# Moving chunk 0's choice of experts from the scatter stage into the dense stage of a hybrid block with product-key experts

## Chip, cores and metric

One NeuronCore of a Trainium2 chip. The metric is the device time of one execution in microseconds; three executions of the kernel before took 1862.81 to 1864.69 us, median 1863.86.

## The reference

One block on 512 tokens of width 1024, in float32: a recurrent branch and an attention branch, mixed and added, and then a layer of 16384 experts addressed by product keys (PEER). The last is what matters here:

```python
def one_chunk(xt):                                  # 128 tokens
    q = (xt @ w_q).reshape(BLOCK, PEER_HEADS, PEER_QDIM)
    s1 = jnp.einsum('chd,nd->chn', q[..., :half], keys1)
    s2 = jnp.einsum('chd,nd->chn', q[..., half:], keys2)
    t1, i1 = lax.top_k(s1, PEER_TOPK)               # 16 of 128
    t2, i2 = lax.top_k(s2, PEER_TOPK)
    cand = t1[..., :, None] + t2[..., None, :]      # 256 candidates
    cidx = i1[..., :, None] * PEER_NKEYS + i2[..., None, :]
    ts, sel = lax.top_k(cand, PEER_TOPK)            # 16 of them
    idx = jnp.take_along_axis(cidx, sel, axis=-1)
    g = jax.nn.softmax(ts, axis=-1)
    act = jax.nn.gelu(jnp.einsum('chkd,cd->chk', u[idx], xt))
    return jnp.einsum('chk,chkd->cd', g * act, v[idx])
```

Each token takes 8 heads x 16 = 128 experts. There are four chunks of 128 tokens. A final norm follows.

## The kernel before

The chunks are handled in the order 1, 2, 3, 0 (`ORDER`). Three of them (1, 2, 3; `NDC = 3`) go through all experts densely: for each of 128 blocks of 128 experts (`NJ`), a u block (24 matmuls of 384 columns, float32 split into a high and a low part) gives activations for 384 tokens, these are multiplied by a matrix of gates, and 18 matmuls with the v block add to six banks `y`. Chunk 0 goes by index: for each of its 128 experts a token the rows of u and then of v are fetched by an indirect DMA on the POOL queue (`fetch`, L913), 128 rows of 4 KB at a time, and VectorE multiplies each with the normed tokens (`first_by_index`, L926) or adds it to `acc` (`second_by_index`, L935). A "row" below is one such fetch and its VectorE operation.

Before the dense stage stand:

- `key_scores` (L724), 16 query products, the top 16 of 128 keys for all four chunks, into `tv` and `ti`;
- `choose` (L757), once per chunk: candidates (a fixed set of 50 pairs of ranks), their top 16 for each of 8 heads (L787 to L791, five operations with a load of match values ahead of three of them), the indices of these by masks (L803 comparison, L805 product, L806 sum), and the gates (L809 difference, L810 Exp on ScalarE, L812 to L814). It is a generator with twelve pieces;
- `scatter` (L843), once per dense chunk: it turns indices and gates into the matrix of gates in DRAM, `gd`, with comparisons on VectorE (L879, L884), scaling on ScalarE (L888), and 128x128 products on TensorE (L869).

`interleave` (L107) runs generators side by side by their weights: each in turn goes on that has used the smallest share of its number of pieces. Scatter of chunk i runs beside the choice of chunk i + 1 and beside u blocks done ahead (`first_ahead`, 41 blocks, `LAG`). Here a scheduler may still move instructions; in the dense stage the context `in_order` keeps VectorE's instructions in the order in which they are written.

In the dense stage `dense` (L971) runs beside the chain of `first_by_index` and `second_by_index`. In step j it first calls `stage(j + 1)` (L952): the u block j + 1 + 41 (two halves, cast on ScalarE L155, difference on VectorE L156; three buffers for what arrives and four for the parts), the v tile (L155, L156; two buffers), and the coefficients `gt`, `ch`, `cl` (L965, L155, L156). Then come the u block's matmuls and the 18 of step j. It yields 4 for a step with a u block (87 of them) and 1 for one without (41); the index chain yields 1 a row, 264 in all. Row buffers: four of 128 x 1024 (`GB = 4`).

```python
yield 1 if w is None else 4
interleave((dense(), 4 * NJ - 3 * LAG), (chain(first_by_index(0), second_by_index(0, acc)), 2 * NS + 2 + GE))
```

Of the kernel before, what the change touches and what calls it, by code (L numbers as in the profile page):

```python
# [19 lines left out]
P = 128  # L20
D = 1024
# [22 lines left out]
NJ = 128  # L44
LAG = 41
# [4 lines left out]
NDC = 3  # L50
# [51 lines left out]
def chain(*gens):  # L102
    for g in gens:
        yield from g


def interleave(*gens):  # L107

    items = [[g, n, 0] for g, n in gens if n]
    while items:  # L110
        it = min(items, key=lambda i: i[2] / i[1])
        try:
            it[2] += next(it[0]) or 1
        except StopIteration:
            items.remove(it)
# [3 lines left out]
def hybrid_block_kernel(ctx: ExitStack, tc, hT, x, win, wkr, vecs, wgate, wrnn, watt, wuq, wukv, wout,  # L119
                        wq, keysT, g2, gf, peer_u, peer_uT, peer_v, cst, out):  # L120
    nc = tc.nc
    V, A, G, TE = nc.vector, nc.scalar, nc.gpsimd, nc.tensor

    def pool(stack, name, side="left", **kw):
        return stack.enter_context(tc.tile_pool(name=name, bufs=1, side=side, reuse_waits="tile", **kw))
# [11 lines left out]
    right = ExitStack()  # L137
# [12 lines left out]
    efx = [cp.tile([P, NS], F32, name=f"efx{c}") for c in range(4)]  # L150
    gate = [cp.tile([P, NS], F32, name=f"gate{c}") for c in range(4)]
# [215 lines left out]
    for hb in range(NK // HB):  # L367
# [47 lines left out]
        ks = [slice(k, k + 1) for k in range(hb * HB, hb * HB + HB)]  # L415
# [297 lines left out]

    dx = ExitStack()
    ctx.enter_context(dx)
    actp = pool(dx, "act", "right")
    vp = pool(dx, "vstream", "right")
    po_ = pool(postx, "choice")
    scx = ExitStack()
    sp_ = pool(scx, "scat", "right")  # L720
    tv = [po_.tile([P, PH, 2, TOPK], F32, name=f"tv{i}") for i in range(4)]
    ti = [po_.tile([P, PH, 2, TOPK], U32, name=f"ti{i}") for i in range(4)]

    def key_scores():  # L724

# [28 lines left out]
            V.max(t[:, 8:16], sv)  # L754
            V.max_index(u[:, 8:16], t[:, 8:16], sv)

    def choose(i, c):  # L757

        work = po_.tile([P, 2 * PH * NCAND], F32, tag="work", bufs=1, name=f"work{c}")
        tf = work[:, PH * NCAND:PH * NCAND + 2 * P].rearrange("p (h a k) -> p h a k", h=PH, a=2)  # L760
        V.tensor_copy(tf, ti[i])
        V.tensor_scalar(tf[:, :, 0, :], tf[:, :, 0, :], float(P), None, op0=OP.mult)
        cd = work[:, :PH * NCAND].rearrange("p (h n) -> p h n", h=PH)
        cx = po_.tile([P, PH, NCAND], F32, tag="cx", bufs=1, name=f"cx{c}")

        def outer(dst, src, a0, na, b0, nb):
            V.tensor_add(dst.rearrange("p h (a b) -> p h a b", b=nb),
                         src[:, :, 0, a0:a0 + na].unsqueeze(3).to_broadcast([P, PH, na, nb]),
                         src[:, :, 1, b0:b0 + nb].unsqueeze(2).to_broadcast([P, PH, na, nb]))

        p0 = 0
        for a0, na, nb in ((0, 1, 16), (1, 1, 8), (2, 1, 5), (3, 1, 4), (4, 1, 3), (5, 3, 2), (8, 8, 1)):
            outer(cd[:, :, p0:p0 + na * nb], tv[i], a0, na, 0, nb)
            p0 += na * nb
            if a0 == 2:
                yield
        yield
        p0 = 0
        for grp in PAIRS:
            for a0, na, b0, nb in grp:  # L780
                outer(cx[:, :, p0:p0 + na * nb], tf, a0, na, b0, nb)
                p0 += na * nb
        yield
        ts = po_.tile([P, PH, TOPK], F32, tag="ts", bufs=1, name=f"ts{c}")
        sel = po_.tile([P, PH, TOPK], U32, tag="sel", bufs=1, name=f"sel{c}")
        for h in range(PH):
            V.max(ts[:, h, 0:8], cd[:, h, :])  # L787
            V.max_index(sel[:, h, 0:8], ts[:, h, 0:8], cd[:, h, :])
            V.match_replace(out=cd[:, h, :], in_to_replace=ts[:, h, 0:8], in_values=cd[:, h, :], imm_value=NEG)
            V.max(ts[:, h, 8:16], cd[:, h, :])  # L790
            V.max_index(sel[:, h, 8:16], ts[:, h, 8:16], cd[:, h, :])  # L791
            if h % 2:
                yield
        sf = po_.tile([P, PH, TOPK], BF16, tag="sf", bufs=1, name=f"sf{c}")
        V.tensor_copy(sf, sel)
        ef = efx[c].rearrange("p (h k) -> p h k", h=PH)
        n = 0
        for g, grp in enumerate(PAIRS):
            n += sum(na * nb for a0, na, b0, nb in grp)
            ks = slice(4 * g, 4 * g + 4)  # L800
            oh = po_.tile([P, PH, 4, NCAND], F32, tag="oh", bufs=1, name=f"oh{c}_{g}")[:, :, :, :n]
            ob = work.bitcast(BF16)[:, :PH * n * 4].rearrange("p (h n k) -> p h n k", h=PH, k=4)
            V.tensor_tensor(ob, sf[:, :, ks].unsqueeze(2).to_broadcast([P, PH, n, 4]),  # L803
                            cand_pos[:, :n].unsqueeze(1).to_broadcast([P, PH, n, 4]), op=OP.is_equal)
            V.tensor_mul(oh, ob.rearrange("p h n k -> p h k n"), cx[:, :, :n].unsqueeze(2).to_broadcast([P, PH, 4, n]))  # L805
            V.reduce_sum(ef[:, :, ks], oh, axis=AX.X)  # L806
            yield
        gw = gate[c].rearrange("p (h k) -> p h k", h=PH)
        V.tensor_sub(gw, ts, ts[:, :, 0:1].to_broadcast([P, PH, TOPK]))  # L809
        A.activation(gate[c], gate[c], AF.Exp)  # L810
        zs = po_.tile([P, PH], F32, tag="zs", bufs=2, name=f"zs{c}")
        V.reduce_sum(zs, gw, axis=AX.X)  # L812
        V.reciprocal(zs, zs)
        V.tensor_mul(gw, gw, zs.unsqueeze(2).to_broadcast([P, PH, TOPK]))  # L814
        yield
# [19 lines left out]
            acts[j] = first_dense(j, ps.tile([P, 512], F32, tag="pt", bufs=2, name=f"a{j}"), w)  # L835
            yield

    cand_pos = sp_.tile([P, NCAND, 4], BF16, name="cand_pos")
    V.tensor_copy(cand_pos, cand_f.unsqueeze(2).to_broadcast([P, NCAND, 4]))
    iota4 = sp_.tile([P, P, 4], BF16, name="iota4")  # L840
    V.tensor_copy(iota4, iota.unsqueeze(2).to_broadcast([P, P, 4]))
# [55 lines left out]
    ga = [first_ahead(a, b) for a, b in zip(ahead, ahead[1:])]  # L897
    na_ = [b - a for a, b in zip(ahead, ahead[1:])]
    interleave((key_scores(), 17), (ga[0], na_[0]))
    interleave((choose(0, ORDER[0]), 11), (ga[1], na_[1]))  # L900
    for i in range(3):
        c = ORDER[i]
        interleave((scatter(i, gate[c], efx[c]), 33), (choose(i + 1, ORDER[i + 1]), 11), (ga[2 + i], na_[2 + i]))
    scx.close()
    postx.close()

# [11 lines left out]

    def first_by_index(c):

        xn2 = xg.tile([P, D], F32, tag="xn2", bufs=1, name=f"xn2_{c}")
        nc.sync.dma_start(xn2, xn2d)
        for s in range(NS):
            t = fetch(peer_u, c, s, f"u{c}_{s}")
            jk = xg.tile([P, D], BF16, tag="jk", bufs=1, name=f"jk{c}_{s}")
            V.scalar_tensor_tensor(jk, t, 1.0, xn2, op0=OP.mult, op1=OP.mult, accum_out=coef[:, s:s + 1])  # L926
            yield
        A.activation(coef, coef, AF.Gelu_apprx_tanh)
        V.tensor_mul(coef, coef, gate[c])
# [17 lines left out]
    acc = fin.tile([P, D], F32, name="acc1")  # L947
# [23 lines left out]
    def dense():  # L971
        for j in range(LAG - LT, LAG):
            acts[j] = first_dense(j, psy.tile([P, 512], F32, tag="pa", bufs=2, name=f"a{j}"), nextw.pop(j, None))
        nxt = stage(0)
        for j in range(NJ):
            w, vh, vl, ch, cl_ = nxt
            if j + 1 < NJ:
                nxt = stage(j + 1)
            if w is not None:
                acts[j + LAG] = first_dense(j + LAG, psy.tile([P, 512], F32, tag="pa", bufs=2, name=f"a{j + LAG}"), w)  # L980
            for i in range(3):
                lh = ch[:, i].rearrange("p q t -> p (q t)")
                ll = cl_[:, i].rearrange("p q t -> p (q t)")
                for nh in range(2):
                    c = slice(nh * 512, (nh + 1) * 512)
                    mm3(yps[i][nh], lh, ll, vh[:, c], vl[:, c], j == 0, j == NJ - 1)
            yield 1 if w is None else 4

    with in_order(tc, *ORD):
        interleave((dense(), 4 * NJ - 3 * LAG), (chain(first_by_index(0), second_by_index(0, acc)), 2 * NS + 2 + GE))  # L990


    yt = {0: acc}
# [102 lines left out]
```

## Time and profile before

| | |
|---|---|
| median of three executions | 1863.86 us |
| the profiled execution | 1864.08 us |
| its span, first to last instruction | 1862.3 us |
| mean granted TensorE clock | 0.994 |
| TensorE busy | 1811.8 us (97%) |
| VectorE busy | 1444.0 us (78%) |
| ScalarE busy | 968.5 us (52%) |
| POOL busy | 355.2 us (19%) |
| transfers | 390.32 MB, mean 210 GB/s |

Busy shares are means over stages; the ends of matmuls are modelled, so "busy" on TensorE says that a matmul was in flight and not that the engine was at its peak. By time: key scores to about 687 us, choices and scatter from there to about 948 us, dense stage to about 1853 us, final norm to the end. The names of the engines in the rows: PE is TensorE, PEld its weight loads, DVE VectorE, ACT ScalarE, SP the queue of most transfers.

### The profile page before, as it was taken

To read this page: it belongs to the slowest core of one execution; us is meant where nothing else is said; L and a number is where in the kernel's file an instruction comes from. 1 tells how busy PE (TensorE), PEld (TensorE's weight loads), DVE (VectorE), ACT (ScalarE), POOL (GpSimd) and SP (SyncE) were. 2 spreads that over 40 slices of the span, in tenths; PEclk is the share of its full clock that TensorE was granted. 3 is DMA by queue.
4 is the path that set the end of the run, shared out by engine and by line. 5 is a ranking of instruction groups with operands and counts; after the bars stand their busy time and mean duration, and the time that the engine had idled before them with its cause. 6 is when DMAs were issued, how large, how long until landed. Compare 5 with 4: busy or idle time off the path is not lost.

```text
span 1862.3 us, 28323 instructions
## 1 busy us (share of the span) xinstructions
PE 1811.8 (97%) x9731; PEld 1601.3 (86%) x9731; DVE 1444.0 (78%) x3088; ACT 968.5 (52%) x2011; POOL 355.2 (19%) x295
## 2 busy tenths in 40 slices
PE   8999999999899999999999999999999999999997
PEld 7888778877778889998999999999999999997886
DVE  7787677777546999997558788877888878887775
ACT  6778576766333337999953333433333333333343
POOL 0100000000100000000014344434444443543310
PEclk9999999999999999999999999999999999999999
DMA  5333212112743223445589999998998989988764
GB/s 163 96 98 105 74 55 66 57 60 75 237 131 125 80 85 125 177 164 193 191 295 336 324 322 352 318 315 307 321 332 310 322 310 322 333 300 272 266 219 153
DMA packets 181600, 390.32 MB, mean 210 GB/s; under 512 B 16593, under 2 KB 68305, under 8 KB 179921
## 3 DMA queue, kind: packets, MB, share of 16 engines
q1 hardware_dynamic: 141632, 245.97, 39.0%
q0 software_dynamic: 39536, 142.00, 22.1%
q8 instruction: 76, 1.25, 0.3%
q10 hardware_dynamic: 288, 0.56, 0.1%
q14 instruction: 68, 0.55, 0.1%
HBM read 353.44 MB, written 34.08 MB: 208 GB/s over the span
## 4 chain that ended last, share of the span: by engine, by line
PE 30%; issue 16%; POOL 6%; DMA 5%; DVE 4%; ACT 1%; DVEq 0%; POOLq 0%; ACTq 0%
PE y L183 5%; PE y L181 5%; PE y L182 5%; PE a L183 4%; POOL v L915 4%; PE a L181 4%; PE a L182 4%; PE sc L869 4%; DMA v<-in_peer_v_dram,eidx 3%; POOL u L915 2%; DMA u<-in_peer_u_dram,eidx 1%; DVE hot L884 1%; DMA gt<-gd 1%; DMA ut_w<-in_peer_uT_dram 0%; DVE ut_l L156 0%
## 5 line engine op out<-in xcount | busy, mean ns | idle before, releaser
L183 PE MATMUL a<-xdh,ut_l 128*128 128x384 f32 x1024 | 347.4, 339 | 9.2 <-DVE ut_l L156 9.2
L181 PE MATMUL a<-xdh,ut_h 128*128 128x384 f32 x1024 | 348.6, 340 | 1.7 <-ACT ut_h L155 1.4
L182 PE MATMUL a<-xdl,ut_h 128*128 128x384 f32 x1024 | 345.5, 337 | 0.3 <-DVE xdl L156 0.3
L155 ACT CAST ut_h<-ut_w 128x512 fp32r<-128x512 f32 x256 | 157.8, 624 | 327.2 <-DMA ut_w<-in_peer_uT_dram 277.9
L181 PE MATMUL y<-vh,ch 128*128 128x512 f32 x768 | 299.6, 390 | 5.4 <-ACT ch L155 5.4
L183 PE MATMUL y<-vh,cl 128*128 128x512 f32 x768 | 301.6, 393 | 0.0
L182 PE MATMUL y<-vl,ch 128*128 128x512 f32 x768 | 301.0, 392 | 0.0
L915 POOL DMA_INDIRECT u<-in_peer_u_dram,eidx x128 | 161.4, 1261 | 666.3 <-DMA gt<-gd 441.4
L915 POOL DMA_INDIRECT v<-in_peer_v_dram,eidx x128 | 175.4, 1370 | 266.8 <-DVE acc L935 239.7
L156 DVE TENSOR_TENSOR ut_l<-ut_w,ut_h 128x512 fp32r<-128x512 f32 x256 | 169.5, 686 | 54.5 <-ACT ut_h L155 51.3
L183 PEld LDWEIGHTS a<-xdh,ut_l 128*128 128x128 f32 x1024 | 194.1, 190 | 11.4 <-DVE ut_l L156 11.0
L181 PEld LDWEIGHTS a<-xdh,ut_h 128*128 128x128 f32 x1024 | 194.3, 190 | 6.1 <-ACT ut_h L155 2.3
L182 PEld LDWEIGHTS a<-xdl,ut_h 128*128 128x128 f32 x1024 | 194.1, 190 | 3.9 <-DVE xdl L156 0.5
L156 DVE TENSOR_TENSOR vl<-vr,vh 128x1024 fp32r<-128x1024 f32 x128 | 157.6, 1232 | 42.9 <-ACT vh L155 41.9
L155 ACT CAST ch<-gt 128x384 fp32r<-128x384 f32 x128 | 65.7, 513 | 232.4 <-DVE gt L965 227.7
L181 PEld LDWEIGHTS y<-vh,ch 128*128 128x128 f32 x768 | 144.7, 188 | 34.8 <-ACT ch L155 6.5
L935 DVE SCALAR_TENSOR_TENSOR acc<-v,coef,acc 128x1024 f32<-128x1024 f32 x128 | 164.1, 1282 | 10.5 <-DMA v<-in_peer_v_dram,eidx 8.5
L183 PEld LDWEIGHTS y<-vh,cl 128*128 128x128 f32 x768 | 144.4, 188 | 31.1 <-DVE cl L156 0.8
L182 PEld LDWEIGHTS y<-vl,ch 128*128 128x128 f32 x768 | 144.5, 188 | 28.5
L926 DVE SCALAR_TENSOR_TENSOR jk<-u,xn 128x1024 bf16<-128x1024 f32 x128 | 156.6, 1223 | 13.7 <-DMA u<-in_peer_u_dram,eidx 11.3
L155 ACT CAST vh<-vr 128x1024 fp32r<-128x1024 f32 x128 | 133.8, 1045 | 32.5 <-PE y L183 28.5
L156 DVE TENSOR_TENSOR cl<-gt,ch 128x384 fp32r<-128x384 f32 x128 | 71.5, 559 | 81.8 <-ACT ch L155 81.8
(348 smaller groups left out, 3470.2 us busy)
## 6 DMA issues: line engine op xcount, KB each, us to landing
ut_w<-in_peer_uT_dram SPq DMA_DIRECT2D x256, 256.0 KB, 6.1
vr<-in_peer_v_dram SPq DMA_DIRECT2D x128, 512.0 KB, 6.7
gd<-stg SPq DMA_DIRECT2D x12, 2048.0 KB, 7.3
gt<-gd SPq DMA_DIRECT2D x96, 256.0 KB, 6.8
wq_w<-in_wq_dram SPq DMA_DIRECT2D x32, 256.0 KB, 2.8
wxr_w<-in_win_dram SPq DMA_DIRECT2D x16, 256.0 KB, 2.8
wgr_w<-in_win_dram SPq DMA_DIRECT2D x16, 256.0 KB, 2.7
wga_w<-in_win_dram SPq DMA_DIRECT2D x16, 256.0 KB, 2.7
```

Source lines behind the costliest of these rows:

```text
L155: A.copy(dst_hi, src)
L156: V.tensor_sub(dst_lo, src, r32(dst_hi))
L181: TE.matmul(o, lh, rh, start=first, stop=False)
L182: TE.matmul(o, lh, rl, start=False, stop=False)
L183: TE.matmul(o, ll, rh, start=False, stop=last)
L869: TE.matmul(o[:, u * P:(u + 1) * P], hot[:, h + u, :], wj[:, h + u, :], start=True, stop=True)
L884: V.tensor_tensor(hot, iota.unsqueeze(1).to_broadcast([P, SG, P]), it[:, t0:t0 + SG].unsqueeze(2).to_broadcast([P, SG, P]), op=OP.is_equal)
L915: G.indirect_dma_start(out=t, out_offset=None, in_=src, in_offset=bass.IndirectOffsetOnAxis(ap=eidx[:, s:s + 1], axis=0))
L926: V.scalar_tensor_tensor(jk, t, 1.0, xn2, op0=OP.mult, op1=OP.mult, accum_out=coef[:, s:s + 1])
L935: V.scalar_tensor_tensor(acc, t, coef[:, s:s + 1], acc, op0=OP.mult, op1=OP.add)
```

## The change

Chunk 0's choice is no longer run beside the scatter of chunk 3. It becomes the head of `first_by_index`, inside the dense stage. Its intermediate tiles are laid into the four row buffers (`row_space`), which are not used before the first fetch; since one row buffer holds 1024 numbers a partition, the product and the sum by masks are made in two halves (`parts = 2`). The top-16 tiles of chunk 0 and the candidates' positions live in a pool that stays open (`keep`). A step with a u block now yields 3 in place of 4, and the index chain counts 275 pieces in place of 264.

```diff
-    tv = [po_.tile([P, PH, 2, TOPK], F32, name=f"tv{i}") for i in range(4)]
-    ti = [po_.tile([P, PH, 2, TOPK], U32, name=f"ti{i}") for i in range(4)]
+    tv = [(po_ if i < NDC else keep).tile([P, PH, 2, TOPK], F32, name=f"tv{i}") for i in range(4)]
+    ti = [(po_ if i < NDC else keep).tile([P, PH, 2, TOPK], U32, name=f"ti{i}") for i in range(4)]
...
-    def choose(i, c):
+    def choose(i, c, space, parts=1):
...
-            oh = po_.tile([P, PH, 4, NCAND], F32, tag="oh", bufs=1, name=f"oh{c}_{g}")[:, :, :, :n]
...
-            V.tensor_mul(oh, ob.rearrange("p h n k -> p h k n"), cx[:, :, :n].unsqueeze(2).to_broadcast([P, PH, 4, n]))
-            V.reduce_sum(ef[:, :, ks], oh, axis=AX.X)
+            m = PH // parts
+            for i in range(parts):
+                hs = slice(i * m, i * m + m)
+                oh = space(f"oh{i}", [P, m, 4, NCAND], F32)[:, :, :, :n]
+                V.tensor_mul(oh, ob[:, hs].rearrange("p h n k -> p h k n"),
+                             cx[:, hs, :n].unsqueeze(2).to_broadcast([P, m, 4, n]))
+                V.reduce_sum(ef[:, hs, ks], oh, axis=AX.X)
...
-    interleave((choose(0, ORDER[0]), 11), (ga[1], na_[1]))
+    choices = [choose(i, c, choice_space(c)) for i, c in enumerate(ORDER[:NDC])] + [iter(())]
+    interleave((choices[0], 11), (ga[1], na_[1]))
...
-        interleave((scatter(i, gate[c], efx[c]), 33), (choose(i + 1, ORDER[i + 1]), 11), (ga[2 + i], na_[2 + i]))
+        interleave((scatter(i, gate[c], efx[c]), 33), (choices[i + 1], 11), (ga[2 + i], na_[2 + i]))
...
-    V.tensor_copy(eidx, efx[0])
...
+        rows = [xg.tile([P, D], F32, tag="row", bufs=GB, name=f"rs{c}_{i}") for i in range(4)]
+        at = dict(work=(0, 0), cx=(1, 0), ts=(1, 400), sel=(1, 528), sf=(1, 656), zs=(1, 720), oh0=(2, 0), oh1=(3, 0))
...
     def first_by_index(c):
 
+        yield from choose(NDC, c, row_space(c), 2)
+        V.tensor_copy(eidx, efx[c])
         xn2 = xg.tile([P, D], F32, tag="xn2", bufs=1, name=f"xn2_{c}")
...
-            yield 1 if w is None else 4
+            yield 1 if w is None else 3
...
-        interleave((dense(), 4 * NJ - 3 * LAG), (chain(first_by_index(0), second_by_index(0, acc)), 2 * NS + 2 + GE))
+        interleave((dense(), 3 * NJ - 2 * LAG), (chain(first_by_index(0), second_by_index(0, acc)), 2 * NS + 13 + GE))
```

TensorE's order stays nearly the same. VectorE's, at the beginning of the dense stage, before: `ut42`, `ut43` are the u blocks of steps 1 and 2, `jk0_0` the product with the first fetched row.

```order
L156 TENSOR_TENSOR vl1_10547<-vr1_10544,vh1_10546 128x1024
L965 TENSOR_TENSOR gt0_10517<-gt0_10517,act1_7313 128x12x32
L156 TENSOR_TENSOR cl1_10552<-gt0_10517,ch1_10551 128x384
L926 SCALAR_TENSOR_TENSOR jk0_0_10604,coef_10418<-u0_0_10602,xn2_0_10600 128x1024
L926 SCALAR_TENSOR_TENSOR jk0_1_10608,coef_10418<-u0_1_10606,xn2_0_10600 128x1024
L926 SCALAR_TENSOR_TENSOR jk0_2_10612,coef_10418<-u0_2_10610,xn2_0_10600 128x1024
L156 TENSOR_TENSOR ut43_l0_10617<-ut43_w0_10614,ut43_h0_10616 128x512
L156 TENSOR_TENSOR ut43_l512_10623<-ut43_w512_10620,ut43_h512_10622 128x512
```

The cast to `eidx` stood eleven rows further up, in front of the dense stage. The same engine after the change, five steps later (`cl5` is the last of step 5's preparation, `ut47` belongs to step 6):

```order
L156 TENSOR_TENSOR cl5_10827<-gt4_10737,ch5_10826 128x384
L817 TENSOR_TENSOR gate0_84<-rs0_1_10506 128x128
L820 TENSOR_REDUCE rs0_1_10506<-gate0_84 128x8
L821 RECIPROCAL rs0_1_10506<-rs0_1_10506 128x8
L822 TENSOR_TENSOR gate0_84<-gate0_84,rs0_1_10506 128x128
L946 CAST eidx_10323<-efx0_80 128x128
L952 SCALAR_TENSOR_TENSOR jk0_0_10885,coef_10324<-u0_0_10883,xn2_0_10881 128x1024
L952 SCALAR_TENSOR_TENSOR jk0_1_10889,coef_10324<-u0_1_10887,xn2_0_10881 128x1024
L156 TENSOR_TENSOR ut47_l0_10894<-ut47_w0_10891,ut47_h0_10893 128x512
```

The index cast now stands directly in front of the product that needs the first fetched row, and the u half of step 6 behind both. The pieces of the choice stand between the preparations of steps 1 to 6, three in step 0 and two or three in each step after it. ScalarE after the change, around the Exp of the gates (`gate0`):

```order
L155 CAST ch5_10826<-gt4_10737 128x384
L155 CAST ut47_h512_10899<-ut47_w512_10897 128x512
L155 CAST ut48_h0_10973<-ut48_w0_10971 128x512
L818 ACT_TABLE_LOAD
L818 ACTIVATE gate0_84<-gate0_84 128x128
L828 ACT_TABLE_LOAD
L828 ACTIVATE act46_10939<-a46_10914 128x384
```

Before, the Exp of chunk 0 stood among the scalings of the scatter stage (`wj1`); now it is behind the casts of two u halves of steps 6 and 7.

## Rows read from the trace of the kernel before

**Rows 1.** Windows: us; busy us of PE, PEld, DVE, ACT, POOL; clock, DMA.

```profile
800.00:850.00 50.00, 47.88 (x331) 47.21 (x329) 47.74 (x148) 48.16 (x128) 0.00 (x0) 0.97 0.40 148
1000.00:1100.00 100.00, 100.00 (x508) 91.08 (x507) 81.34 (x128) 36.50 (x60) 42.07 (x33) 1.00 0.93 320
1740.00:1780.00 40.00, 40.00 (x178) 33.11 (x178) 30.09 (x38) 15.67 (x20) 12.36 (x7) 1.00 0.78 267
```

**Rows 2.** PE in time, 935 to 943 us: start us, us, line, operation.

```profile
935.16 3.73 PE L869 MATMUL sc<-wj,hot 128*128 128x128 f32 x32
938.65 0.42 PE L181 MATMUL a<-xdh,ut_h 128*128 128x384 f32 x1
...
942.90 3.73 PE L869 MATMUL sc<-wj,hot 128*128 128x128 f32 x32
```

**Rows 3.** Groups on PE, 873 to 946 us: xcount | busy us, mean ns.

```profile
L869 PE MATMUL sc<-wj,hot 128*128 128x128 f32 x252 | 30.1, 275 | 0.0
L181 PE MATMUL a<-xdh,ut_h 128*128 128x384 f32 x86 | 29.6, 344 | 0.0
L183 PE MATMUL a<-xdh,ut_l 128*128 128x384 f32 x87 | 29.2, 336 | 0.0
```

**Rows 4.** Windows of 10 us in the scatter stage, columns as in rows 1.

```profile
830.00:840.00 10.00, 8.60 (x60) 8.09 (x59) 9.90 (x50) 9.99 (x28) 0.00 (x0) 1.00 0.52 210
840.00:850.00 10.00, 9.28 (x55) 9.12 (x55) 9.06 (x11) 9.28 (x26) 0.00 (x0) 0.83 0.23 80
870.00:880.00 10.00, 8.75 (x55) 8.11 (x54) 7.67 (x11) 9.97 (x27) 0.00 (x0) 1.00 0.81 290
```

**Rows 5.** Tile `work` of the choices: ns min/median/max, first and last start.

```profile
L761 DVE CAST work<-ti x4: 276/286/290, 687.4 to 812.5; 128x256 f32<-128x256 uint32 x4
```

**Rows 6.** DVE in time, first dense steps; in brackets the idle time before.

```profile
965.89 1.23 DVE L926 SCALAR_TENSOR_TENSOR jk<-u,xn 128x1024 bf16<-128x1024 f32 x1 [0.33 <-DMA u<-in_peer_u_dram,eidx]
...
970.84 1.29 DVE L156 TENSOR_TENSOR ut_l<-ut_w,ut_h 128x512 fp32r<-128x512 f32 x2
...
974.84 1.22 DVE L926 SCALAR_TENSOR_TENSOR jk<-u,xn 128x1024 bf16<-128x1024 f32 x1
```

**Rows 7.** Groups by form, 850 to 960 us, ScalarE's part of chunk 0's choice.

```profile
L810 ACT ACT_TABLE_LOAD x1 | 1.3, 1283 | 0.0
...
L810 ACT ACTIVATE gate<-gate 128x128 f32<-128x128 f32 x1 | 0.3, 310 | 0.0
```

**Rows 8.** Instructions of DVE in time, the first choice (chunk 1).

```profile
687.37 0.28 DVE L761 CAST work<-ti 128x256 f32<-128x256 uint32 x1
...
690.40 1.89 DVE L767 TENSOR_TENSOR cx<-work 128x32 f32<-128x32 f32 x20
692.21 0.31 DVE L787 MAX8 ts<-work 128x8 f32<-128x50 f32 x2
...
693.79 0.67 DVE L156 TENSOR_TENSOR ut_l<-ut_w,ut_h 128x512 fp32r<-128x512 f32 x1
```

**Rows 9.** Groups by form, 700 to 850 us, operations of the choice.

```profile
L805 DVE TENSOR_TENSOR oh<-work,cx 128x1600 f32<-128x1600 bf16 x3 | 5.5, 1818 | 0.0
...
L790 DVE MAX8 ts<-work 128x8 f32<-128x50 f32 x26 | 4.4, 204 | 0.0
...
L788 DVE MATCH_VALUE_LOAD sel<-ts,work 128x8 f32 x26 | 2.1, 82 | 0.0
...
L805 DVE TENSOR_TENSOR oh<-work,cx 128x256 f32<-128x256 bf16 x4 | 1.7, 425 | 0.1
```

**Rows 10.** PE in time: the first matmul of step 2's u block.

```profile
973.46 0.33 PE L181 MATMUL a<-xdh,ut_h 128*128 128x384 f32 x1
```

**Rows 11.** DMA issues, 850 to 940 us: xcount, KB each, median us to landing.

```profile
ut_w<-in_peer_uT_dram SPq DMA_DIRECT2D x29, 256.0 KB, 3.1
```

**Rows 12.** DMA issues, 950 to 1100 us.

```profile
ut_w<-in_peer_uT_dram SPq DMA_DIRECT2D x37, 256.0 KB, 7.0
```

**Rows 13.** Instructions of POOL in time: the first fetch of a row.

```profile
957.32 1.00 POOL L915 DMA_INDIRECT u<-in_peer_u_dram,eidx  x1 [441.42 <-DMA gt<-gd]
```

More of the change, by code (lines that the diff above doesn't have):

```diff
@@ L715, in hybrid_block_kernel @@
     ctx.enter_context(dx)
+    keep = pool(dx, "keep", "right")
     actp = pool(dx, "act", "right")
@@ L755, in scores, with choice_space @@
             V.max_index(u[:, 8:16], t[:, 8:16], sv)
-    def choose(i, c):
-        work = po_.tile([P, 2 * PH * NCAND], F32, tag="work", bufs=1, name=f"work{c}")
+    def choice_space(c):
+        return lambda tag, shape, dt: po_.tile(shape, dt, tag=tag, bufs=1, name=f"{tag}{c}")
+    def choose(i, c, space, parts=1):
+        work = space("work", [P, 2 * PH * NCAND], F32)
         tf = work[:, PH * NCAND:PH * NCAND + 2 * P].rearrange("p (h a k) -> p h a k", h=PH, a=2)
@@ L763, in choose @@
         cd = work[:, :PH * NCAND].rearrange("p (h n) -> p h n", h=PH)
-        cx = po_.tile([P, PH, NCAND], F32, tag="cx", bufs=1, name=f"cx{c}")
+        cx = space("cx", [P, PH, NCAND], F32)
         def outer(dst, src, a0, na, b0, nb):
@@ L783, in choose @@
         yield
-        ts = po_.tile([P, PH, TOPK], F32, tag="ts", bufs=1, name=f"ts{c}")
-        sel = po_.tile([P, PH, TOPK], U32, tag="sel", bufs=1, name=f"sel{c}")
+        ts = space("ts", [P, PH, TOPK], F32)
+        sel = space("sel", [P, PH, TOPK], U32)
         for h in range(PH):
@@ L793, in choose @@
                 yield
-        sf = po_.tile([P, PH, TOPK], BF16, tag="sf", bufs=1, name=f"sf{c}")
+        sf = space("sf", [P, PH, TOPK], BF16)
         V.tensor_copy(sf, sel)
@@ L810, in choose @@
         A.activation(gate[c], gate[c], AF.Exp)
-        zs = po_.tile([P, PH], F32, tag="zs", bufs=2, name=f"zs{c}")
+        zs = space("zs", [P, PH], F32)
         V.reduce_sum(zs, gw, axis=AX.X)
@@ L836, in first_ahead @@
             yield
-    cand_pos = sp_.tile([P, NCAND, 4], BF16, name="cand_pos")
+    cand_pos = keep.tile([P, NCAND, 4], BF16, name="cand_pos")
     V.tensor_copy(cand_pos, cand_f.unsqueeze(2).to_broadcast([P, NCAND, 4]))
@@ L910, in hybrid_block_kernel, with row_space, space @@
     coef = xg.tile([P, NS], F32, name="coef")
-    V.tensor_copy(eidx, efx[0])
+    def row_space(c):
+        rows = [xg.tile([P, D], F32, tag="row", bufs=GB, name=f"rs{c}_{i}") for i in range(4)]
+        at = dict(work=(0, 0), cx=(1, 0), ts=(1, 400), sel=(1, 528), sf=(1, 656), zs=(1, 720), oh0=(2, 0), oh1=(3, 0))
+        def space(tag, shape, dt):
+            i, a = at[tag]
+            n = int(np.prod(shape[1:])) // (2 if dt == BF16 else 1)
+            t = rows[i][:, a:a + n]
+            t = t if dt == F32 else t.bitcast(dt)
+            if len(shape) == 2:
+                return t
+            names = "abc"[:len(shape) - 1]
+            return t.rearrange(f"p ({' '.join(names)}) -> p {' '.join(names)}", **dict(zip(names, shape[1:])))
+        return space
     def fetch(src, c, s, name):
```

## Prediction

> **What bounds the kernel now.** I read the windows by stage first. From about 960 us on, TensorE is the bound: in 100 us it runs 508 matmuls at 100% busy and full clock, while VectorE is busy 81 and ScalarE 37 of 100 us [rows 1]. A step with a u block has 42 matmuls, so it takes 42 / 508 x 100 = 8.27 us. In the stage before, 800 to 850 us, three engines are nearly full: TensorE 47.9, VectorE 47.7, ScalarE 48.2 of 50 us. A stage with three full engines says little about which of them ends last, so I asked what TensorE could do at best there. In order of time one tile of 32 scatter products and one u block of 24 matmuls together take 942.90 - 935.16 = 7.74 us, 3.49 for the 32 products and 4.25 for the 24 [rows 2]. From 873 to 946 us the trace has 252 products and 259 u matmuls, 86, 87 and 86 (two of the three groups are shown) [rows 3]; at those rates they need 27.5 + 45.9 = 73.4 of the 73 us. TensorE is at its own pace there, and no relief of VectorE can gain anything. What can be gained is only where it stands still: in slices of 10 us these are 830 to 850 and 870 to 880, with 1.40 + 0.72 + 1.25 = 3.4 us of standing still, and a mean granted clock of 0.83 in one slice, part of it at the lower level (1.2 GHz), worth 0.17 x 10 = 1.7 us [rows 4]. Chunk 0's choice, the last of four, runs from 812 us on [rows 5], so these slices lie in it and just behind it. **The most that taking it out can bring is 5.1 us.**
>
> **The dense stage before.** VectorE's instructions run in written order here. In each step it prepares the next step (two halves of the u block, the v tile, the coefficients): 970.84 to 974.84, 4.0 us [rows 6]. Then come two or three row products of about 1.25 us. 4.0 + 2.7 x 1.25 = 7.4 of 8.27 us, so in a step it has less than 1 us to spare, and it works one step ahead of TensorE. Both are too little for what follows.
>
> **The change, part by part.** Removed from the scatter stage: the choice on VectorE, and on ScalarE an Exp and its two table loads, 0.31 + 2 x 1.28 = 2.9 us [rows 7]. ScalarE was at 48.2 of 50, so without this it could be the next bound; with it taken out I credit the whole 5.1 us.
>
> Added to the dense stage: the choice in twelve pieces, ahead of the first row. It replaces the rows of the first five steps. What it costs there, from chunk 1's choice in order of time [rows 8]: the cast and the sums for the candidates 3.03 us from 687.37 to 690.40, less three u halves that lie between them at 0.6 each, so 1.2; the index sums 1.8 (690.40 to 692.21). The top-16 of two heads took 1.58 us there, but the five operations of one head alternated with the other's. In the new order each head stands alone and each operation waits for the one ahead of it. One head has five operations of 0.20 and three value loads of 0.08 [rows 9]: 1.24, with its small gaps 1.3 us. So I take 1.3 for a head against 0.79 in the trace, and keep 0.79 as the lower end: 8 x 0.51 = 4.1 us over the choice. The Trainium skill, VectorE: DVE Perf Modes, section The DRAIN you can't avoid, states that a semaphore after each operation costs nothing extra; by it the heads would stay at 0.79 and the time would be some 4 us shorter. The trace speaks against it for these short operations, which start before the one ahead has ended when they don't need it.
>
> The selection by masks: a multiplication takes 0.425 us for 256 elements and 1.818 for 1600 [rows 9], so 0.16 + 0.00104 per element, and the reduction as much. Done in two halves, a group has one comparison and four such operations of half the size: groups of 256, 640, 1120 and 1600 elements come to 1.5, 2.5, 3.7 and 4.9 us (comparisons 0.3, 0.5, 0.7, 0.99).
>
> **The walk.** VectorE is free after step 1's preparation at 965.89 - 0.33 = 965.5 [rows 6]. TensorE needs the first u half of step 2 at its third matmul, 973.46 + 0.35 = 973.8 [rows 10], and that of each later step 8.27 us on.
> Step 0: 3.0 us of sums, then the preparation of step 2 until 972.5; in time.
> Step 1: six heads, 7.8, until 980.3; the u half is ready 0.7 later, 981.0, due 982.1; in time. Preparation until 984.3.
> Step 2: two heads 2.6, cast 0.25, first two groups 4.0, until 991.1; ready 991.8, due 990.4: **TensorE waits 1.4**. Preparation until 995.1.
> Step 3: last two groups 8.6, until 1003.7; ready 1004.4, due 991.8 + 8.27 = 1000.1: **it waits 4.3**. Preparation until 1007.7.
> Step 4: the gate. The Exp stands on ScalarE behind the cast of a u half whose transfer can be issued only when VectorE has freed its buffer, at 1005.0. It lands 3.1 us later by the transfers of the scatter stage, when no rows were fetched [rows 11], or 7.0 later by those of the dense stage [rows 12]; I take 3.1, since no rows are fetched in these steps, and keep 7.0 as the other end. With cast, table load and Exp (0.6 + 1.3 + 0.3) and 1.0 for VectorE's sum, reciprocal, product and the cast to indices, the indices are there at 1011.3 (1015.2). Only now can POOL fetch. Before, its first fetch started at 957.32 and VectorE's first product at 965.89, held until then by the transfer [rows 6, 13]: 8.6 us. If a fetch gains from quiet queues as the u halves do, it takes 8.6 x 3.1 / 7.0 = 3.8, 4.8 less; I keep that as its lower end, and take the 8.6, the one row that measures this very path. In the new order the product stands directly behind the index cast, so VectorE is idle all that time, and the preparation of step 6 is queued behind it. Two rows, 2.5, until 1022.4; the u half is ready 1023.1 (1027.0), due 1012.7: **TensorE waits 10.4 (14.3)**.
> The Trainium skill, DMA: Bandwidth & Descriptors, section Anatomy of one DMA, gives 2.0 us plus bytes / 436e3 for a transfer by this path, an estimate of 3.2 us for 512 KB; with it in place of 8.6 the last wait would be 5.4 shorter. The row of this kernel says 8.6.
>
> Sum of waits 1.4 + 4.3 + 10.4 = 16.1 us (20.0). After the last and longest one the clock falls as in rows 4: 1.7 more. What the clock costs after the second wait is nothing, since the third ends when VectorE is ready, not when TensorE comes. 16.1 + 1.7 - 5.1 = **+12.7 us**. The profiled execution took 1864.08 us, 0.2 above the median, so 1876.6 for the median, 1877 rounded.
>
> **Costed at nothing.** The rows of the later steps: up to the last steps with u there are still two or three per step, and in the 40 steps after them 32 instead of 20. In 40 us of that part (178 / 18 = 9.9 steps) VectorE is busy 30.1 us [rows 1]; 0.3 more rows a step are 0.3 x 9.9 x 1.25 = 3.7, so 34 of 40, and with 0.3 x 0.52 MB more in 4.04 us, on 267 GB/s, the share of transfers goes from 0.78 to about 0.89. That cover is thin: a transfer that comes late is no longer caught up. The index chain ends some steps before the dense one in the new order too, so the end is still TensorE's. The cast of the candidate positions only moves ahead. The buffers of the choice are row buffers and lie idle then.
>
> **Rivals.**
> *Faster: the spare time takes it.* VectorE is idle 19% of the dense stage [rows 1], some 16 us in ten steps, and a step ahead. If row products and choice were spread over those, only the 5.1 us would be left: 1859. Against it stands the fixed order, which sets the waits step by step and not by the average. Deciding point: step 6's u half is due at 973.8 + 4 x 8.27 = 1006.9 if nothing waited; 8.6, 2.5 and 0.7 lie between it and the index cast, so VectorE would have to be there by 995. 6%.
> *No difference.* The heads cost 0.79 (4.1 less), the fetch 3.8 (4.8 less) and the clock stays up (1.7): 12.7 - 10.6 = +2.1, 1866. Each alone is possible, all three hardly. 6%.
> *Slower for a second reason.* The u halves land after 7.0, and ScalarE, almost full, lets the scatter stage gain only 2: 20.0 + 1.7 - 2 = +19.7, 1884. 14%.
> *The last steps become bound by transfers or VectorE*, at 32 rows in place of 20: a late row every ten steps costs about 2 us and a fallen clock, 3 x 3.7 = 11 on top, 1888. Nothing in the part before shows such waits in number. 4%.
> *The change doesn't unload the scatter stage*: the second slot there could stay as full, with the other chunks' choices moved into its time. Then +17.8, 1882; I count it with the slower cases above.
>
> **How the numbers follow.** Forecast 70%, rivals 6, 6, 14 and 4. From no change a measurement of this kernel can tell 0.2%, 3.7 us. Faster 0.06, within 0.06, slower 0.88. The range must hold 80%: its lower end is the forecast with the cheap heads and the shorter fetch, 12.7 - 8.9 = +3.8, 1867 and a half; the upper end takes in the 1884 and some of the last case, 1887.
>
> **What would show it.** Right: TensorE's waits on the u half from VectorE in the first six dense steps, one of about 10 us among them; VectorE's longest wait then on the first u row, of 7 us or more; no standing still of TensorE around 830 to 850; the Exp of chunk 0 behind a cast of a u half; dense steps from the eighth on at 8.27 us as before. Wrong: if TensorE's waits in the first eight steps come to under 8 us, the prices of the choice or the one-step lead are wrong; if the scatter stage shortens by more than 5 us, its matmuls were not at their own pace; if TensorE waits in the last 40 steps in more places than before, the thin cover was one.

## The result and the profile after

The changed kernel takes 1877.78 us (median of six runs, 1870.81 to 1880.47), the kernel before beside it 1862.30 (1859.85 to 1864.69): a ratio of 1.0079 with a 95% interval of 1.0059 to 1.0100. It is slower, by 15.5 us between the medians (11 to 19 by the interval). The forecast was 1877.0. The profiled execution spans 1874.8 us, 12.5 more than the one before.

The windows of the changed kernel, columns as in [rows 1] (start and end; busy us of PE, PEld, DVE, ACT, POOL; clock; transfers). Line numbers differ from kernel to kernel.

```profile
800.00:850.00 50.00, 49.39 (x349) 48.67 (x348) 35.39 (x48) 48.67 (x132) 0.00 (x0) 1.00 0.48 168
830.00:840.00 10.00, 9.78 (x69) 9.37 (x69) 5.87 (x8) 9.97 (x28) 0.00 (x0) 1.00 0.51 208
840.00:850.00 10.00, 9.61 (x67) 9.30 (x66) 5.68 (x7) 10.00 (x30) 0.00 (x0) 1.00 0.43 127
860.00:870.00 10.00, 9.42 (x66) 8.98 (x65) 4.90 (x8) 9.76 (x29) 0.00 (x0) 1.00 0.56 218
870.00:880.00 10.00, 10.00 (x67) 9.81 (x66) 6.42 (x10) 9.45 (x27) 0.00 (x0) 1.00 0.57 184
960.00:1000.00 40.00, 35.96 (x180) 31.98 (x178) 35.96 (x132) 13.69 (x21) 0.00 (x0) 1.00 0.48 151
1000.00:1040.00 40.00, 33.05 (x147) 30.48 (x148) 27.49 (x47) 11.82 (x18) 14.87 (x14) 0.87 0.79 264
1016.00:1020.00 4.00, 2.92 (x9) 2.92 (x10) 3.37 (x7) 0.51 (x1) 1.14 (x1) 0.50 1.01 338
1020.00:1024.00 4.00, 4.00 (x17) 3.95 (x16) 3.93 (x6) 0.85 (x2) 1.86 (x2) 0.66 0.72 266
1100.00:1200.00 100.00, 97.99 (x493) 87.95 (x491) 79.10 (x123) 36.38 (x60) 42.17 (x33) 1.00 0.92 315
1740.00:1780.00 40.00, 40.00 (x177) 32.80 (x176) 32.20 (x40) 15.67 (x20) 14.24 (x9) 1.00 0.86 292
```

The first row answers to the first of [rows 1]: VectorE is relieved (47.7 to 35.4 of 50 us), TensorE goes from 47.9 to 49.4 and its clock from 0.97 to 1.00. ScalarE goes from 48.2 to 48.7 and is nearly full. Chunk 0's Exp never stood in this window: before, it ran at 862 us. The slices of [rows 4] are nearly closed, 0.6 us of standing still in place of 3.4, but 860 to 870 has 0.6 that it lacked before. The loss stands in 960 to 1040 us: TensorE stands still for 4.0 + 7.0 us, and a clock of 0.87 over 40 us is 5.2 more.

What TensorE waited for, 940 to 1060 us, by group (us in total, times, longest), and then the three waits in order of time, the idle time before in brackets. `a` are the products of a u block, `y` those of a v block; `ut_l` is VectorE's part of a u block, `ch` ScalarE's cast of the coefficients, `act` its Gelu of a finished u block:

```profile
PE a L183 <- DVE ut_l L156: 11.0, 3, 6.1
PE y L181 <- ACT ch L155: 1.6, 1, 1.6
```

```profile
988.41 0.44 PE L183 MATMUL a<-xdh,ut_l 128*128 128x384 f32 x1 [1.41 <-DVE ut_l L156]
1000.84 0.44 PE L183 MATMUL a<-xdh,ut_l 128*128 128x384 f32 x1 [3.48 <-DVE ut_l L156]
1017.08 0.69 PE L183 MATMUL a<-xdh,ut_l 128*128 128x384 f32 x1 [6.11 <-DVE ut_l L156]
```

All three are for the u half of VectorE, in the steps that the walk named. VectorE in the same stretch, in order of time: the start of two heads that follow each other, the gate's sum, the cast to indices, the first two row products. Then POOL's first fetch, and the coefficient product of dense step 0, after and before.

```profile
969.14 0.20 DVE L791 MAX8 rs<-rs 128x8 f32<-128x50 f32 x1
...
970.45 0.19 DVE L791 MAX8 rs<-rs 128x8 f32<-128x50 f32 x1
...
1006.49 0.29 DVE L820 TENSOR_REDUCE rs<-gate 128x8 f32<-128x128 f32 x1 [2.15 <-ACT gate L818]
...
1007.26 0.22 DVE L946 CAST eidx<-efx 128x128 int32<-128x128 f32 x1
1012.80 1.23 DVE L952 SCALAR_TENSOR_TENSOR jk<-u,xn 128x1024 bf16<-128x1024 f32 x1 [5.32 <-DMA u<-in_peer_u_dram,eidx]
...
1015.19 1.23 DVE L952 SCALAR_TENSOR_TENSOR jk<-u,xn 128x1024 bf16<-128x1024 f32 x1 [1.16 <-DMA u<-in_peer_u_dram,eidx]
```

```profile
1008.34 1.00 POOL L939 DMA_INDIRECT u<-in_peer_u_dram,eidx  x1 [491.99 <-ACT act L828]
```

```profile
956.40 0.56 DVE L991 TENSOR_TENSOR gt<-gt,act 128x384 f32<-128x384 f32 x1 [5.14 <-DMA gt<-gd]
959.91 0.57 DVE L965 TENSOR_TENSOR gt<-gt,act 128x384 f32<-128x384 f32 x1 [5.28 <-DMA gt<-gd]
```

A head takes 970.45 - 969.14 = 1.31 us. From the fetch to the product are 1012.80 - 1008.34 = 4.5 us, in place of the 8.6 of [rows 6, 13], and the second row comes 1.2 late as well.

### The profile page after: what moved, and what is told of

It reads as the page before. It is cut to its first block, busy times and chain, and to the rows that moved or that the text cites. A ratio compares the mean times of both kernels' runs of the same rounds, so it can differ in the third digit from the quotient of the medians.

```text
span 1874.8 us, 28321 instructions
## 1 busy us (share of the span) xinstructions
PE 1815.5 (97%) x9731; PEld 1601.1 (85%) x9731; DVE 1448.0 (77%) x3096; ACT 967.7 (52%) x2011; POOL 358.1 (19%) x295
## 4 chain that ended last, share of the span: by engine, by line
PE 69%; DVE 10%; DMA 7%; issue 7%; ACT 5%; POOL 2%; SPq 0%; DVEq 0%; ACTq 0%; POOLq 0%
PE y L183 7%; PE y L181 7%; PE y L182 7%; PE a L183 7%; PE a L181 7%; PE a L182 7%; PE sc L877 4%; DMA u<-in_peer_u_dram,eidx 3%; PE q L181 2%; PE q L182 2%; PE q L183 2%; PE wgn_ps L228 2%; PE wgr_ps L228 2%; POOL u L939 2%; DMA wo_w<-in_wout_dram 2%
```

## The experiments

Each set of runs had the kernel before beside it on its own chip. Its median there lay between 1862.6 and 1866.7 us, so ratios are compared, not times.

**Is the result the same on another chip?** The changed kernel again, unaltered.

> The changed kernel once more, on the chip of the experiments, so that they can be set against it there. My theory: the same ratio to the kernel before as in the first measurement, 1.006 to 1.010; waits of TensorE on u halves of about 1.4, 3.5 and 6.1 us between 985 and 1020. Rival, chips differ in it: a ratio of 1.002 to 1.005, and then what the experiments gained is less than it seems.

Ratio 1.0068 (1.0047 to 1.0089), waits of 1.39, 3.48 and 4.92 us. The first number stands. The last wait is shorter here only because TensorE came later: its clock was at 0.50 from 1004 to 1008 us. Counted from the coefficient product of dense step 0, the late u half is used after 1019.27 - 958.63 = 60.64 us here and after 1017.08 - 956.40 = 60.68 in the first trace. VectorE sets that point. What the clock cost TensorE before it, it would have waited anyway.

**What is the relief of the scatter stage worth alone?** The kernel before:

```diff
-        interleave((scatter(i, gate[c], efx[c]), 33), (choose(i + 1, ORDER[i + 1]), 11), (ga[2 + i], na_[2 + i]))
+        interleave((scatter(i, gate[c], efx[c]), 33),
+                   (choose(i + 1, ORDER[i + 1]) if i < 2 else iter(()), 11), (ga[2 + i], na_[2 + i]))
...
```

> The kernel before with chunk 0's choice left out: its row stage uses chunk 3's weights and indices instead, as many rows and bytes, so the output of chunk 0 is another one. It prices the relief of the scatter stage alone. My theory: TensorE there is at its own pace but for 3.4 us of standing still and 1.7 us of clock, so the time falls by 3.4 to 5.1 us, to 1857 to 1859 us, the coefficient product of dense step 0 starts about 3.5 us earlier than at 959.91 (as it did in the changed kernel, 956.40), and TensorE has no wait over 0.5 us from 800 to 950. Rival, ScalarE is the next bound: a fall of 2 us or less, 1860 to 1862, with TensorE still waiting on ScalarE's copies there. Rival, the whole choice was on the path: its 30 us of VectorE work would give 10 us or more, under 1852.

Ratio 0.9986 (0.9973 to 0.9999), some 2.6 us (0.2 to 5.0). From 800 to 850 us TensorE is busy 49.42 us at a clock of 1.00, as in the changed kernel. Dense step 0's product starts at 954.34. Over all traces of this study it starts at 957.75 to 959.91 (mean 958.8, three) with the choice in the scatter stage and at 953.19 to 959.24 (mean 955.8, eleven) without: 3.0 us, but the two ranges overlap. Much of their width is there before the first choice, which starts anywhere from 684.8 to 689.5 us. Counted from that start, step 0 comes 271.2 to 272.6 us later with the choice (mean 271.8) and 267.3 to 269.8 without (mean 268.3): 3.5 us, and no overlap. So my 5.1 was too much; that all of the 30 us of work was on the path is out, and by this count so is the rival of 2 us or less, which the ratio alone leaves open. This trace gives its lead back at the last u blocks:

```profile
PE y L181 <- ACT ch L155: 4.7, 2, 3.9
PE a L181 <- ACT act L820: 1.6, 1, 1.6
```

**Is the long wait the preparation queued behind the fetch?** Two ways to part them in the changed kernel. First the products one step later:

```diff
         nc.sync.dma_start(xn2, xn2d)
+        for _ in range(3):
+            yield
```

> The changed kernel, with the first row product written one dense step later, so that the preparation of the next step stands between the cast to indices and the first product; nothing else moves. My theory: the 6.1 us wait of TensorE is the preparation queued behind the fetch (4.5 us from the fetch to the product) and goes whole, with some of the 5.2 us that the clock of 0.87 cost from 1000 to 1040: 6 to 9 us less than the changed kernel, 1869 to 1872; the waits of 1.4 and 3.5 us stay. Rival, VectorE is simply too late by then from the choice, or the u half is late by itself: the wait only moves on to a later step, 1875 to 1879.

Ratio 1.0018 (1.0004 to 1.0032), 9 to 11 us less than the changed kernel by the two ratios of that, a little more than expected. The waits are 1.38, 3.49 and 0.76:

```profile
PE a L183 <- DVE ut_l L156: 5.6, 3, 3.5
PE y L181 <- ACT ch L155: 1.3, 1, 1.3
```

Second, only the cast to indices earlier:

```diff
-        yield from choose(NDC, c, row_space(c), 2)
-        V.tensor_copy(eidx, efx[c])
+        for k, _ in enumerate(choose(NDC, c, row_space(c), 2)):
+            if k == 10:
+                V.tensor_copy(eidx, efx[c])
+            yield
```

> The changed kernel, with only the cast to indices written directly behind the last masks, ahead of one preparation and of the weights' part (subtraction, Exp, sum, reciprocal, product); the order of the rest stays. My theory: the fetch then runs beside that preparation, and the first product no longer holds the next one up: of the waits 1.4 and 3.5 us stay and 6.1 goes to 1 or less, with the 3.4 us that the clock costs behind it; a ratio of 1.001 to 1.004. Rival, what holds is ScalarE's Exp (2.2 us of VectorE's wait): a wait of 2 to 3 us stays, 1.004 to 1.006.

Ratio 1.0039 (1.0023 to 1.0054), waits of 1.41, 3.74 and 1.20 us:

```profile
1012.33 0.44 PE L183 MATMUL a<-xdh,ut_l 128*128 128x384 f32 x1 [1.20 <-DVE ut_l L156]
```

In both the long wait falls to about 1 and the clock is at 1.00 from 1012 us on. It was the preparation behind the fetch. These runs also show what the fetch takes. VectorE and POOL in the first of them:

```profile
1010.22 0.22 DVE L946 CAST eidx<-efx 128x128 int32<-128x128 f32 x1
...
1019.10 1.23 DVE L954 SCALAR_TENSOR_TENSOR jk<-u,xn 128x1024 bf16<-128x1024 f32 x1 [3.70 <-DMA u<-in_peer_u_dram,eidx]
```

```profile
1011.29 1.22 POOL L939 DMA_INDIRECT u<-in_peer_u_dram,eidx  x1 [493.33 <-ACT act L828]
```

Here a preparation with its transfers runs beside the fetch, and it takes 1019.10 - 1011.29 = 7.8 us. In the four traces where the fetch runs with little beside it (the 16 DMA engines 0.53 to 0.61 busy meanwhile) it takes 4.2 to 4.6 us, the 4.5 above among them; in seven (0.80 to 1.05) it takes 7.8 to 8.9, among them this run and the 8.6 of before. The busy share isn't the whole of it: the three runs of the spread choice with rows behind, below, have 5.4 to 6.6 us to the landing at 0.75 to 1.04.

**Is it the size of the pieces?** The changed kernel with the choice over more steps:

```diff
-        yield from choose(NDC, c, row_space(c), 2)
+        for _ in choose(NDC, c, row_space(c), 2):
+            yield 2
...
```

> The changed kernel, with each piece of the choice counted twice, so that its twelve pieces lie over some nine dense steps in place of five; the rows behind it come a little denser. My theory: the waits come from pieces larger than the 4.3 us that a step leaves VectorE, so those of 1.4 and 3.5 us go and what is left is at most 3 us, where the last masks stand with the gate or at the first rows, and the clock stays up: 8 to 14 us less than the changed kernel, 1864 to 1870. Rival, all of the loss is the fetch: the 6 us wait stays, 1872 to 1875. Rival, the denser rows behind cost as much again: no wait in the first ten steps but others later, 1875 or more.

No wait of TensorE at all from 960 to 1100 us, not even at the fetch, since VectorE has its step of lead again. But the ratio is 1.0030 (1.0014 to 1.0046). TensorE's waits from 1300 to 1720 us:

```profile
PE y L181 <- ACT ch L155: 5.6, 2, 4.8
PE a L181 <- ACT act L828: 5.1, 5, 2.6
```

So my theory holds for the first steps. Behind them 2.8 rows stand in a step in place of 2.7, as the rival of the denser rows had it; this run alone does not show that they are the cause.

**Does a head alone cost 1.3 us because it is alone?** In the changed kernel two heads in turn, `MAX8` of one, `MAX8` of the other, and so on:

```diff
-        for h in range(PH):
-            V.max(ts[:, h, 0:8], cd[:, h, :])
+        for h in range(0, PH, 2):
+            for k in (h, h + 1):
+                V.max(ts[:, k, 0:8], cd[:, k, :])
...
```

> The changed kernel, with the five operations of two heads written in turn (one of the first head, the same of the second) in place of head by head. My theory: a head alone takes 1.30 us because each of its operations waits for the one before; in turn two take 1.58 as in the stage before, so the choice is 4.1 us shorter, and as VectorE sets the end of all three waits their sum falls from 11.0 to about 7, 4 to 5 us less than the changed kernel, 1872 to 1874. Rival, the operations take that long by themselves: two heads stay at 2.6 us, and the time does not change, 1876 to 1879.

```profile
970.00 0.32 DVE L793 MAX8 rs<-rs 128x8 f32<-128x50 f32 x2
...
971.59 0.30 DVE L793 MAX8 rs<-rs 128x8 f32<-128x50 f32 x2
...
973.16 0.31 DVE L793 MAX8 rs<-rs 128x8 f32<-128x50 f32 x2
```

Two heads take 1.58 us, 0.79 each, by the same instructions. The ratio is 1.0033 (1.0019 to 1.0048), 6.5 to 8.6 us less than the changed kernel by the two ratios of that, more than the 4 to 5 expected; the spans of the two traces differ by 3.9. The waits come to 8.8 us, and not 7, since TensorE, less delayed in between, stands 7.4 at the last.

**Do the later rows cost nothing?** Only the changed kernel's weight of the dense steps, in the kernel before, and then the opposite, with 30 in place of 3 and the total to match:

```diff
-            yield 1 if w is None else 4
+            yield 1 if w is None else 3
...
-        interleave((dense(), 4 * NJ - 3 * LAG),
+        interleave((dense(), 3 * NJ - 2 * LAG),
```

> The kernel before, with only the change's weights of the dense steps (3 in place of 4, so that more rows fall in the last 40 steps); the choice stays in the scatter stage. My theory: later rows cost nothing and bring nothing, a ratio of 0.998 to 1.002. Rival, fewer rows per step with u blocks take away the stop of TensorE near 1690 us (2.8 us and a fallen clock in the trace of before, 0.5 in the changed kernel's): 0.996 to 0.998. Rival, the last steps become tight: over 1.002, with waits of TensorE after 1700 us.

> The kernel before, with only the weight of the dense steps changed (30 in place of 4): all 256 rows fall in the steps with u blocks, three in nearly each (2.98 a step, where before had 2.71 and the run with the change's weights 2.62). My theory: the density of rows costs, since a step then has 4.0 + 3.75 of 8.27 us of VectorE and more transfers, and a late transfer is no longer caught up: 2.62 a step gained 0.14%, so 2.98 should lose 0.3 to 0.6%, a ratio of 1.003 to 1.006, with waits of TensorE on VectorE or ScalarE between 1000 and 1640 us, where the kernel before has 2.8 us. Rival, the spare time of VectorE is enough at any density under 3.4: 0.998 to 1.002.

With 2.62 rows a step with a u block (before: 2.71) the ratio is 0.9986 (0.9975 to 0.9998), inside what I gave; with 2.98 it is 1.0142 (1.0126 to 1.0157). The stop near 1690 us stays in the first (4.0 us in all after 1640), so the rival that hung on it falls. In the second the loss is two to five times what I gave. Waits from 1100 to 1640 us there:

```profile
PE a L181 <- ACT act L820: 16.0, 14, 2.0
DVE jk L926 <- DMA u<-in_peer_u_dram,eidx: 14.7, 18, 2.1
DVE acc L935 <- DMA v<-in_peer_v_dram,eidx: 13.9, 22, 1.5
DVE ut_l L156 <- ACT ut_h L155: 12.3, 12, 1.7
DVE vl L156 <- ACT vh L155: 10.2, 17, 0.6
```

A step takes 8.65 us there (the coefficient products of steps 14 and 84 start at 1075.09 and 1680.27), so these 540 us are 62 steps. VectorE waits 28.6 / 62 = 0.46 us in each for rows to land and 22.5 / 62 = 0.36 for ScalarE's casts. With 4.0 of preparation and three products 1.27 apart that is 8.63: VectorE is full and sets the step.

**All repairs together.** The changed kernel with heads in pairs, the choice over eight steps (the largest group of masks cut in two), indices before the gate and the rows behind them, run twice:

```diff
...
+            if k == 11:
+                V.tensor_copy(eidx, efx[c])
+            yield STEPS[k]
...
+    STEPS = (.1, 2.7, 1.4, 1.4, 1.4, 1.4, 1.4, 1.4, 2.8, 2.8, 2.8, 2.8, 2.8)
```

> The changed kernel with all three put together: heads in pairs, the choice over eight dense steps with no piece above 4 us (the largest group of masks cut in two), the cast to indices directly behind the masks and the first row product two steps behind it. My theory: no wait of TensorE over 1.5 us in the first twelve dense steps and its clock at 1.00 there, so that only the scatter stage's gain is left: a ratio to the kernel before of 0.997 to 1.000 (leaving the choice out altogether gave 0.9986). Rival, the denser rows behind (up to three in each step) bring back waits after 1300 us: 1.002 to 1.005, with TensorE's waits there 4 us or more. Rival, the choice's work itself costs in the dense stage wherever it stands: 1.004 to 1.006.

> The run with all three put together once more: its profiled execution was the fastest of twelve, 6 us under their median, and tells nothing of the slower ones. My theory: the median comes out at a ratio of 1.000 to 1.003 again, and a profiled execution near the median has waits of TensorE between 1040 and 1720 us that the fast one lacks, 5 us or more, behind late transfers, and none in the first twelve dense steps. Rival, the slower executions lose it ahead of the dense stage or in the first steps: then a later start of dense step 0 than 953.2, or waits there.

Ratios 1.0016 (1.0001 to 1.0031) and 1.0007 (0.9997 to 1.0016). No wait from 960 to 1100 us in either. The first profiled execution, a span of 1856.8 us, was the fastest of twelve and has none up to 1640; the second, 1864.2, has 3.6 us for ScalarE's `act` there. Up to 1720 us it has 4.2 more than the first, a little under the 5 that I gave. The rival has its part too: dense step 0 starts 2.2 us later in it (955.36 against 953.19), and this difference is there before the first choice. So the theory of the first steps holds, and a part of the gain is eaten behind them, where 2.82 rows stand in a step (2.84 without the first step, which has one); whether they are the cause is what the next run asks. Fewer rows there, with weights of 2:

> The kernel of the run with all three put together (choice spread, heads in pairs, index cast early), with weights of 2 for the dense steps in place of 3: 205 rows in the 77 steps with u blocks that have rows (2.66 a step, there 2.82) and 51 in the last 41 steps. My theory: what kept that kernel from the scatter stage's gain was the density of its rows, so now it comes: a ratio of 0.997 to 1.000. Rival, the last steps become tight with 51 rows: waits of TensorE after 1700 us of 4 us or more, 1.002 to 1.005. Rival, the choice costs 3 to 5 us wherever it stands in the dense stage: again 1.001 to 1.003, without waits in the last steps.

```profile
1300.00:1640.00 340.00, 340.00 (x1721) 309.21 (x1720) 275.70 (x356) 127.01 (x205) 142.18 (x109) 1.00 0.92 317
1740.00:1780.00 40.00, 34.71 (x148) 27.43 (x149) 31.72 (x37) 12.67 (x18) 17.86 (x11) 1.00 0.87 304
```

```profile
PE y L181 <- ACT ch L155: 20.0, 13, 1.9
```

Ratio 1.0061 (1.0047 to 1.0074). With 2.66 rows a step TensorE never waits up to 1640 us, and then 13 times in the last steps: there a step lasts 4.04 us, and a preparation without u halves (1.22 + 0.55 + 0.56) with two products (2.5) is 4.8. That rival came true. It suggests one row in a late step and about 2.7 in one with a u block.

**Fitted between.** The same kernel (heads in pairs, indices early) with the choice in seven steps and no group of masks cut, the gate's Exp ahead of the masks, and a weight of 2.72:

```diff
...
-            yield 1 if w is None else 3
+            yield 1 if w is None else 2.72
...
+    STEPS = (.1, .1, 2.5, 1.4, 1.4, 1.4, 1.4, .1, 2.6, 2.7, 4.4)
```

> The kernel of the runs with all three put together, fitted between what they showed: the choice over seven dense steps (the weights' subtraction and Exp ahead of the masks, their sum and product two groups later), one row in the first step with rows, then 2.74 a step in the steps with u blocks (2.88 in the first of those runs, 2.66 in the run with weights of 2, which had no wait up to 1640 us but 20 us of waits behind it) and exactly one in nearly each of the last 41. My theory: the choice is hidden, the last steps have room for one row each, and the density is that of the kernel before: a ratio of 0.995 to 0.999, the scatter stage's gain kept, with no wait of TensorE on u halves in the first twelve dense steps. Rival, seven steps are too few for the choice: waits of 2 us or more there, 1.000 to 1.003. Rival, one row in each of the last steps is as tight as 51 in all: waits of 4 us or more after 1720 us, 1.001 to 1.004.

```profile
800.00:850.00 50.00, 49.37 (x344) 48.57 (x343) 35.36 (x49) 49.14 (x133) 0.00 (x0) 1.00 0.48 169
960.00:1000.00 40.00, 40.00 (x204) 36.35 (x203) 36.38 (x139) 19.02 (x29) 0.00 (x0) 1.00 0.58 187
1000.00:1040.00 40.00, 40.00 (x205) 36.51 (x204) 30.89 (x48) 14.06 (x22) 18.04 (x14) 1.00 0.85 288
1640.00:1720.00 80.00, 80.00 (x376) 68.95 (x375) 64.30 (x74) 29.18 (x41) 33.47 (x23) 1.00 0.88 303
1740.00:1780.00 40.00, 40.00 (x178) 33.11 (x177) 33.66 (x41) 14.91 (x20) 17.64 (x10) 1.00 0.93 313
```

1855.53 us against 1864.51, a ratio of 0.9959 (0.9943 to 0.9976): faster than both kernels. From 960 us to the end of the last step TensorE has no recorded wait. Against the trace before, 10.7 us of span are gone: dense step 0 starts 959.91 - 953.83 = 6.1 earlier, and the stop near 1690 us is absent, 2.8 us and a clock that from 1640 to 1720 stood at 0.98 there (1.6 us). This trace is the fastest of its six; by the ratio the gain is 7.6 us, and 1.6 of the 6.1 lie before the first choice, where the kernels do the same. Which of this kernel's edits took the stop near 1690 away was not tried; most runs with other spacing have it. Leaving the choice out altogether gave 0.9986, so part of 0.9959 is likely the spacing of the rows and not the choice.

## Why the prediction was right

The direction, the mechanism and the sum held: +12.7 us predicted, +12.5 by the spans. The gain of the scatter stage and the fetch were put too large and the clock too small, and two effects left at nothing cancel in this pair of traces, so part of the agreement is luck. Of its signs, the long wait was to be about 10 us and is 6.1, VectorE's wait at the first u row 7 or more and is 5.3.

*The scatter stage*: 5.1 at most and taken whole; 3.5 by step 0's start in this pair (959.91 to 956.40), and 3.5 over all traces, counted from the first choice.

*The walk of VectorE*: right up to the indices. I put them at 1011.3 from a start of 959.91, 51.4 later; the cast ends at 1007.26 + 0.22 = 1007.48, 51.1 after 956.40. Heads of 1.3 and waits of 1.4 and 4.3 came out as 1.31, 1.41 and 3.48. The Trainium skill, VectorE: DVE Perf Modes, section The DRAIN you can't avoid, states that a semaphore after each operation costs nothing extra, from which the prediction worked out 0.79 for a head in any order; the runs show 1.31 alone and 0.79 in pairs, so here the measurement decides against it. The Exp stood behind casts of u halves, as I said, but neither of them waited for its transfer: the gate's sum was held 2.15 us by the casts, the table load and the Exp itself.

*The fetch*, the step that was mis-sized: I took 8.6 from the one row of before, with 3.8 as the other end. It took 4.5, with 1.2 more for the second row, and POOL began it only 0.9 after the cast, which the walk left out. The u half was used 60.7 after the start, where the prediction had 1023.1 - 959.9 = 63.2, and the wait was 6.1 in place of 10.4, also because the clock had by then delayed TensorE by 1.7. The Trainium skill, DMA: Bandwidth & Descriptors, section Anatomy of one DMA, gives an estimate of 3.2: nearer to the quiet 4.5, far from the 7.8 beside other transfers. My own argument, that in these steps few transfers run, was there and I didn't follow it.

*The clock*: 1.7 after the last wait; the rows from 1016 to 1024 us show 0.50 and 0.66 over 4 us each, 2.0 + 1.4 = 3.4. The fall after the second wait, some 1.7 from 1000 to 1008 us, cost nothing, as I argued: the run on another chip shows it. The sum below counts it all the same, because the wait behind it was measured shorter by about as much.

*Later rows at nothing*: not so. The changed kernel has 2.3 us of waits behind ScalarE's `act` from 1100 to 1300 us, which before lacks, and lacks most of the stop near 1690, 2.3 us and its clock (1.6). These nearly balance in this pair of traces; in the second trace of the changed kernel they are 1.1 us of waits and a stop of 1.9. The number of rows doesn't explain the waits: a step with a u block has 2.71 of them in both kernels. Their cause stays open. The cover in the last steps, called thin, held: from 1740 to 1780 us VectorE is busy 32.2 us, transfers at 0.86, and after 1720 TensorE waits 0.8 us in both kernels. It breaks with more rows there (20.0 us). The density of rows by itself moves the time from 0.9986 to 1.0142, more than the change did.

In all: -3.5 in the scatter stage, +11.0 of waits, +5.2 of clock, +2.3 behind, -3.9 at the end of the u blocks make +11.1 of the 12.5. The starts of the u blocks in the two traces show where the rest is: after the change the 17th (1106 us) starts 12.4 later than before, the 39th (1293 us) 16.2 later. That stretch cost 3.8 us, where its recorded waits come to 2.3.

The rival *faster* was not wrong in what it needed. VectorE's idle time does carry the choice, if it is dealt out step by step; the change as it was written didn't do that.

## What to carry to other kernels

Work that is moved into an engine with a fixed order must be cut to what a single step leaves free, and no instruction that waits for a fetch should stand ahead of the next step's preparation. An average of idle time says nothing on either. Where every step is nearly full, the spacing of the filler work is worth measuring by itself: here 0.27 rows a step more cost 1.4%, and moving the choice 0.8%. Short operations that depend on one another should be written in turns with those of another chain.

## What was not expected of the hardware

The same row fetch takes 4.2 to 4.6 us with little other traffic (DMA engines 0.53 to 0.61 busy) and mostly 7.8 to 8.9 beside a step's transfers (0.80 to 1.05). And VectorE's short selection operations take the same 0.20 us each whether alone or in turns, but a chain of five lasts 1.31 us alone and 0.79 in turns.
